# The last stage of a decoder block, turned round: per-layer embedding, its gate and the final norm with tokens on the partitions

## The chip, the core and the metric

The kernel runs on one core of a Trainium2 chip. TensorE multiplies matrices (in the profile PE, and PEld for its weight loads), VectorE (DVE) and ScalarE (ACT) work element by element, GpSimd (POOL) and SyncE (SP) here mostly issue transfers. The metric is the device time of one execution in microseconds (us); the profile gives the span from the first to the last instruction of one profiled execution.

## What is computed

One layer on 512 tokens of width 1024, all in float32. The change touches only the last lines of the reference:

```
    h = h + 0.5 * swiglu(rms_norm(h, g_ffn2), w_ffn2_gate, w_ffn2_up, w_ffn2_down)

    gate = jax.nn.sigmoid(rms_norm(h, g_ple) @ w_ple_gate)     # (512, 1024) @ (1024, 1024)
    h = h + gate * (p @ w_ple_proj)                            # (512, 256) @ (256, 1024)
return rms_norm(h, g_final)
```

## The kernel before

All activations lie with features on the partitions: h is eight tiles (`KD = 8`) of 128 features x 512 tokens in the big tile `gx`. A float32 product is made of three matmuls of the faster type fp32r, because each operand is split into a high part rounded to fp32r and a remainder (names ending in h and l): `mm3` (lines 337 to 339) issues high x high, high x low, low x high. In a matmul row of the profile the first name is the operand that moves and the second the one that is loaded as weights: `pg<-xsh,pgh 128*128 128x256` moves 256 tokens of `xsh` past 128 x 128 of `pgh`.

Weights come in slabs of 128 x 1024 floats (512 KB). `slab_order` writes their order down; `slab(key)` hands one out and on the way issues the loads some seven slabs ahead (`load_one`, from SP's queue, line 190) and the splits two slabs ahead (`split_one`). For the gate matrix, key `("pg", m)`, a split is two halves of 512 columns: ACT writes `pgh` (line 304), DVE subtracts to give the half of `wl` (line 305). Loads wait for a free buffer among 19, which the matmuls of the second feed-forward give back. Every engine takes its instructions in the order in which the program writes them.

The stage around the change runs after the second feed-forward's last down-projection (tiles `pd`). While that ends, `into(V_GP, gs, gnorm, h)` makes `gs` (`xsh`, `xsl`: h times the gain g_ple, split) and sums the squares of h in `gnorm`. Then:

1. The projection `pp` (L337 to L339 with 512 tokens moving): 8 output tiles of 128 features, 6 matmuls each, copied out of PSUM by ACT (L1089). Inside it `gnorm.by_token()` finds 1/rms of each token with small matmuls against `mean` (L450) and a dozen tiny DVE operations (L456 to L462).
2. The gate, in two halves of 256 tokens, 8 output tiles `m` each, 24 matmuls of 256 columns per tile. The 1/rms of a token varies along a row here, so it is spread over all partitions by one matmul (`on_all`, L471 and L477: tile `R`) and multiplied in by DVE (`gate`, L1122) ahead of the Sigmoid (L1123).
3. `add_on`, one tile later: times `pp` (L1129), plus h (L1130), times the gain g_final into `hg` (L1131), squares for the final norm (L428, L436, L1139).
4. `fnorm[half].by_token(...)` for the final norm, `turn_out`: 32 transposes of 128 x 128 of `hg` on PE (L1101) to put tokens on the partitions, and `put_out`: times 1/rms out of PSUM by DVE (L1110) and ACT (L1108), 256 KB a transfer to `out` from SP's queue (L1112). The first half's part lies beside the second half's matmuls; the second half's comes after the last matmul.

The splits of the gate's slabs stand in the same two instruction streams as steps 2 and 3: at tile `m` of the first half the program writes the split of slab `m + 2`, then the work on tile `m`, then `add_on` of tile `m - 1`.

Of the kernel before, what the change touches and what calls it, by code (L numbers as in the profile page):

```python
# [12 lines left out]
I32 = mybir.dt.int32  # L13
# [114 lines left out]
def block_kernel(ctx: ExitStack, tc: tile.TileContext, a, out):  # L128
# [7 lines left out]
    psum = ctx.enter_context(tc.tile_pool(name="psum", bufs=1, space=PSUM))  # L136
    ctx.enter_context(tc.manual_schedule())
# [26 lines left out]
    def source(key):  # L164
# [21 lines left out]
    def fetch(*srcs, first_=False):  # L186

        r, at = W("wh", F32R) if first_ else W("wr"), 0
        for src in srcs:
            (G if first_ else nc.sync).dma_start(r[:, at:at + src.shape[-1]], src)  # L190
            at += src.shape[-1]
        return r[:, :at]
# [226 lines left out]

    class Norm:  # L420
# [18 lines left out]
        def by_token(self, lo=0, hi=NB, more=()):  # L439
            n = hi - lo  # L440
            every = [self.acc] + list(more)
# [3 lines left out]
            ps = [bank("ss") for _ in range(n if more else 1)]  # L445
            pairs = [(i, b) for b in range(n) for i in range(len(every))]
            if more:
                pairs.sort()
            for i, b in pairs:
                PE.matmul(ps[b % len(ps)][:, b:b + 1], every[i][:, b * P:(b + 1) * P], mean[:, 0:1], start=i == 0,  # L450
                          stop=i == len(every) - 1)
            m, y, t = (small.tile([P, NB], F32, name=name(q), tag="nt" + q, bufs=2) for q in "myt")
            m, y, t = m[:, :n], y[:, :n], t[:, :n]
            w = n // len(ps)
            for i, p in enumerate(ps):
                V.tensor_scalar(m[:, i * w:(i + 1) * w], p[:, i * w:(i + 1) * w], EPS, None, op0=OP.add)  # L456
            V.tensor_scalar(t.bitcast(I32), m.bitcast(I32), 1, None, op0=OP.logical_shift_right)
            V.tensor_scalar(y.bitcast(I32), t.bitcast(I32), -1.0, MAGIC, op0=OP.mult, op1=OP.add)
            for _ in range(3):
                V.tensor_mul(t, m, y)  # L460
                V.scalar_tensor_tensor(t, t, -0.5, y, op0=OP.mult, op1=OP.mult)
                V.scalar_tensor_tensor(y, t, 1.5, y, op0=OP.add, op1=OP.mult)  # L462
            if n == NB:
# [611 lines left out]

    pTh, pTl = slab(("pT",))
    pp = []
    for j in range(2):
        wh, wl = slab(("pp", j))
        for i in range(4):  # L1080
            if j and i == 1:
                gnorm.by_token()
            p = bank("pp")
            for kk in range(2):
                c = slice((2 * i + kk) * P, (2 * i + kk + 1) * P)
                z = slice(kk * S, (kk + 1) * S)
                mm3(p, wh[:, c], wl[:, c], pTh[:, z], pTl[:, z], kk == 0, kk == 1)
            t = T("pp")
            A.activation(t, p, AF.Copy)  # L1089
            pp.append(t)  # L1090
    pTh = pTl = wh = wl = None
    H = S // 2
    kept = []
    fin = []

    def turn_out(half, m):

        for b in range(2):
            if m % 4 == 0:
                fin[half][b].append(bank("py"))  # L1100
            PE.transpose(fin[half][b][m // 4][:, (m % 4) * P:(m % 4 + 1) * P], hg[half][m][:, b * P:(b + 1) * P], ident)  # L1101

    def put_out(half, r):
        for b in range(2):
            for c in range(2):
                y = T("y")
                if c:
                    A.activation(y, fin[half][b][c], AF.Copy, scale=r[:, b:b + 1])  # L1108
                else:
# [133 lines left out]
```

## Time and profile before

| | |
|---|---|
| time, median of 3 runs (lowest to highest) | 1329.42 us (1329.3 to 1331.38) |
| the profiled execution: its own time | 1330.73 us |
| the profiled execution: span | 1329.0 us |
| mean granted TensorE clock over the span | 0.996 of 2.4 GHz |
| PE busy, share of the span | 99% |
| DVE, ACT, POOL busy, share of the span | 63%, 52%, 17% |

Times in the profile count from the start of the span. Busy time of a matmul is a model that overlaps its neighbours; how fast matmuls follow one another is read from their start times. The stage of the change covers about the last 75 us: the projection from about 1254, the gate from 1264.86, its last matmul at 1316.41, the end at 1329.0.

### The profile page before, as it was taken

To read this page: it belongs to the slowest core of one execution; us is meant where nothing else is said; L and a number is where in the kernel's file an instruction comes from. 1 tells how busy PE (TensorE), PEld (TensorE's weight loads), DVE (VectorE), ACT (ScalarE), POOL (GpSimd) and SP (SyncE) were. 2 spreads that over 40 slices of the span, in tenths; PEclk is the share of its full clock that TensorE was granted. 3 is DMA by queue.
4 is the path that set the end of the run, shared out by engine and by line. 5 is a ranking of instruction groups with operands and counts; after the bars stand their busy time and mean duration, and the time that the engine had idled before them with its cause. 6 is when DMAs were issued, how large, how long until landed. Compare 5 with 4: busy or idle time off the path is not lost.

```text
span 1329.0 us, 19593 instructions
## 1 busy us (share of the span) xinstructions
PE 1311.4 (99%) x7636; PEld 1168.7 (88%) x7636; DVE 843.8 (63%) x1405; ACT 685.0 (52%) x958; POOL 220.1 (17%) x290
## 2 busy tenths in 40 slices
PE   8999999999999999999999999999999999999997
PEld 6899899898888898989898888888899899898897
DVE  5986467352449877777688956654983366352665
ACT  5567276564522355555464244343676367474553
POOL 3111111112232222222122210001112011111000
PEclk9999999999999999999999999999999999999999
DMA  9678756959888776767577792235479576868601
GB/s 286 140 174 215 198 139 171 244 139 222 199 207 192 166 180 143 157 146 160 133 159 182 169 243 79 95 95 127 115 181 238 164 172 176 225 160 217 178 1 64
DMA packets 78716, 221.05 MB, mean 166 GB/s; under 512 B 8864, under 2 KB 9760, under 8 KB 78624
## 3 DMA queue, kind: packets, MB, share of 16 engines
q0 software_dynamic: 41184, 135.28, 49.3%
q1 hardware_dynamic: 37440, 84.52, 18.6%
q8 instruction: 60, 0.98, 0.3%
q14 instruction: 32, 0.26, 0.1%
HBM read 166.29 MB, written 2.10 MB: 127 GB/s over the span
## 4 chain that ended last, share of the span: by engine, by line
PE 86%; DVE 6%; issue 3%; ACT 2%; DMA 1%; POOL 0%; SPq 0%; DVEq 0%; ACTq 0%; POOLq 0%
PE pd L337 8%; PE pd L339 8%; PE pd L338 8%; PE pa L337 6%; PE pa L339 6%; PE pa L338 6%; PE pg L339 3%; PE pg L338 3%; PE pg L337 3%; PE pq L338 3%; PE pq L337 3%; PE pq L339 3%; PE pv L961 2%; PE pb L337 2%; PE pb L339 2%
## 5 line engine op out<-in xcount | busy, mean ns | idle before, releaser
L264 POOL DMA_DIRECT2D wl<-wr x102 | 89.4, 877 | 508.9 <-ACT wl L261 465.3
L777 DVE SCALAR_TENSOR_TENSOR acc<-glu,taps,acc 128x511 f32<-128x511 f32 (+14 forms) x240 | 165.1, 733 | 0.0
L337 PE MATMUL pd<-hidh,wh 128*128 128x512 f32 x352 | 137.2, 390 | 0.0
L338 PE MATMUL pd<-hidl,wh 128*128 128x512 f32 x352 | 137.2, 390 | 0.0
L339 PE MATMUL pd<-hidh,wl 128*128 128x512 f32 x352 | 137.1, 389 | 0.0
L261 ACT ACTIVATE wl<-wr 128x1024 fp32r<-128x1024 f32 (+1 forms) x102 | 103.9, 1019 | 55.7 <-DMA wr<-in_w_ffn_gate 22.0
L337 PE MATMUL pa<-bh,wh 128*128 128x256 f32 x432 | 122.6, 284 | 1.7 <-ACT p L624 1.7
L339 PE MATMUL pa<-bh,wl 128*128 128x256 f32 x432 | 122.6, 284 | 0.0
L338 PE MATMUL pa<-bl,wh 128*128 128x256 f32 x432 | 122.4, 283 | 0.0
L339 PE MATMUL pg<-xsh,wl 128*128 128x512 f32 (+1 forms) x320 | 111.5, 349 | 0.6 <-DVE wl L305 0.4
L277 ACT ACTIVATE wh<-wr 128x1024 fp32r<-128x1024 f32 (+1 forms) x102 | 103.5, 1014 | 15.4 <-DMA wl<-wr 13.0
L297 DVE TENSOR_TENSOR wl<-s,wh 128x1024 fp32r<-128x1024 f32 x54 | 66.0, 1223 | 68.2 <-ACT wh L296 68.1
L661 DVE SCALAR_TENSOR_TENSOR gx<-pd,gx 128x512 f32<-128x512 f32 x48 | 33.1, 691 | 113.0 <-PE pd L339 112.9
L261 ACT ACTIVATE wl<-wh 128x1024 fp32r<-128x1024 f32 (+1 forms) x84 | 84.3, 1010 | 24.3 <-DMA wh<-in_w_in 15.7
L264 POOL DMA_DIRECT2D wl<-in_w_in x56 | 48.7, 870 | 233.0 <-ACT wl L261 219.5
L337 PEld LDWEIGHTS pa<-bh,wh 128*128 128x128 f32 x432 | 83.0, 192 | 2.1 <-ACT p L624 2.1
L339 PEld LDWEIGHTS pa<-bh,wl 128*128 128x128 f32 x432 | 83.0, 192 | 0.1
L338 PEld LDWEIGHTS pa<-bl,wh 128*128 128x128 f32 x432 | 83.0, 192 | 0.0
L337 PE MATMUL pd<-bh,wh 128*128 128x256 f32 x288 | 82.0, 285 | 0.5 <-ACT p L624 0.4
L338 PE MATMUL pd<-bl,wh 128*128 128x256 f32 x288 | 81.6, 283 | 0.0
L339 PE MATMUL pd<-bh,wl 128*128 128x256 f32 x288 | 81.6, 283 | 0.0
L337 PE MATMUL pg<-xsh,wh 128*128 128x512 f32 x192 | 77.2, 402 | 2.2 <-ACT xsh L357 2.2
(258 smaller groups left out, 3687.0 us busy)
## 6 DMA issues: line engine op xcount, KB each, us to landing
wl<-wr POOLq DMA_DIRECT2D x86, 512.0 KB, 6.7
wh<-in_w_in POOLq DMA_DIRECT2D x56, 512.0 KB, 6.7
wl<-in_w_in POOLq DMA_DIRECT2D x56, 512.0 KB, 5.6
wr<-in_w_ffn_up SPq DMA_DIRECT2D x80, 256.0 KB, 5.0
wr<-in_w_ffn_gate SPq DMA_DIRECT2D x78, 256.0 KB, 5.1
wr<-in_w_ffn_down SPq DMA_DIRECT2D x32, 512.0 KB, 5.7
wr<-in_w_ffn_down SPq DMA_DIRECT2D x16, 384.0 KB, 5.6
wl<-wr POOLq DMA_DIRECT2D x16, 384.0 KB, 6.7
```

The lines of the kernel that those rows point to most:

```text
L261: A.activation(l.bitcast(F32R), h, AF.Copy, scale=-1.0)
L264: G.dma_start(l[:, at:at + src.shape[-1]], src, accum_op=OP.add)
L277: A.activation(h, r, AF.Copy)
L297: V.tensor_sub(l, r, h.bitcast(F32))
L337: PE.matmul(ps, wh, xh, start=start, stop=False, skip_group_check=part)
L338: PE.matmul(ps, wh, xl, start=False, stop=False, skip_group_check=part)
L339: PE.matmul(ps, wl, xh, start=False, stop=stop, skip_group_check=part)
L661: V.scalar_tensor_tensor(resid[m], p, 0.5, resid[m], op0=OP.mult, op1=OP.add)
L777: bg.append(lambda acc=acc, g=g, w=w, s=s: V.scalar_tensor_tensor(acc[:, s:], g[:, :S - s], w, acc[:, s:], op0=OP.mult, op1=OP.add))
L961: PE.matmul(pv[b][:, :384], xh, wh[:, c], start=first_, stop=False)
```

## The change

The same products with the two operands swapped: the activations are loaded as weights (128 tokens at a time) and the weight matrix moves, 512 columns at a time, so the result has tokens on the partitions. There are four blocks `b` of 128 tokens, and for each two column halves `j` of 512 features.

- A slab of the gate matrix is now 128 input features x all 1024 outputs: the same 512 KB, read as 1024 pieces of 512 bytes (eight to a partition) where it was 128 rows of 4 KB.
- Block 0 runs over the slabs as the outer loop, both `j` side by side, six matmuls to a slab; the split parts stay in SBUF for blocks 1 to 3.
- 1/rms is now one number per partition: `by_token(diag=False)` leaves out the `diag` tiles, `on_all` goes, and the Sigmoid reads PSUM and takes 1/rms as its scale. DVE's multiplication by `R` goes.
- h is turned instead of the output: 32 transposes of h on PE (`turned`, L1117), eight ahead of block 0, four in the middle of each later unit; DVE adds them from PSUM.
- `close` does a unit's element-wise work; the squares for the final norm come out of one ACT instruction with a sum along the row (`accum_out`). `root` is the tiny chain of DVE operations, once a block; `put_out` of a block stands behind the next block's first unit. The last unit (block 3, j = 1) is cut into two of 256 columns.
- g_final is needed along a row: 1024 numbers are read from the input `gx`, one four-byte element at a time, into a row in DRAM (`row`), and from there copied to all partitions (two tiles `gf` of 256 KB). These three transfers stand in SP's queue.

```
+        if kind == "pg":
+            return a["w_ple_gate"][:, :, key[1] * P:(key[1] + 1) * P].rearrange("m p i -> p m i")
...
+    row, gf = dram.tile([1, D], F32, name="row"), [T("gf") for _ in range(2)]
+    nc.sync.dma_start(row.rearrange("o (c p e) -> o c p e", c=KD, e=1), bass.AP(
+        tensor=a["gx"].tensor, offset=a["gx"].offset + V_GF, ap=[[0, 1], [1, KD], [V_DW + S, P], [1, 1]]))
+    for c in range(2):
+        nc.sync.dma_start(gf[c], row[0:1, c * S:(c + 1) * S].partition_broadcast(P))
...
-                mm3(p, wh[:, c], wl[:, c], pTh[:, z], pTl[:, z], kk == 0, kk == 1)
+                z = slice(kk * S + b * P, kk * S + (b + 1) * P)
+                PE.matmul(p, pTh[:, z], wh[:, kk], start=kk == 0, stop=False)
+                PE.matmul(p, pTl[:, z], wh[:, kk], start=False, stop=False)
+                PE.matmul(p, pTh[:, z], wl[:, kk], start=False, stop=kk == 1)
...
+    def products(units, ks=range(KD)):
+        for k in ks:
+            for b, j, z, p in units:
+                xh, xl = (t[:, b * P:(b + 1) * P] for t in gs[k])
+                wh, wl = (t[j][:, z] for t in kept[k])
+                p = p[:, :z.stop - z.start]
+                PE.matmul(p, xh, wh, start=k == 0, stop=False)
+                PE.matmul(p, xl, wh, start=False, stop=False)
+                PE.matmul(p, xh, wl, start=False, stop=k == KD - 1)
+
+    def turned(b, j, z):
+        p = bank("hT", "cv")
+        for i in range(z.start // P, z.stop // P):
+            PE.transpose(p[:, i * P - z.start:(i + 1) * P - z.start], h[4 * j + i][:, b * P:(b + 1) * P], ident)
+        return p
+
+    def close(b, j, z, p, hT):
+        w = z.stop - z.start
+        t, u = T("gt")[:, :w], T("hg")[:, :w]
+        A.activation(t, p[:, :w], AF.Sigmoid, scale=r[:, b:b + 1])
+        V.tensor_mul(t, t, pp[b, j][:, z])
+        V.tensor_add(t, t, hT[:, :w])
+        part = tiny("part", 1)
+        A.activation(u, t, AF.Square, scale=D ** -0.5, accum_out=part)
+        V.tensor_mul(t, t, gf[j][:, z])
+        if b in sums:
+            V.tensor_add(part, part, sums[b])
+        else:
+            V.tensor_scalar(part, part, EPS, None, op0=OP.add)
+        sums[b] = part
...
+    def put_out(b):
+        y = sums.pop(b)
+        for i, (t, c, w) in enumerate(done.pop(b)):
+            if i % 2:
+                V.tensor_scalar(t, t, y, None, op0=OP.mult)
+            else:
+                A.activation(t, t, AF.Copy, scale=y)
+            nc.sync.dma_start(out[b * P:(b + 1) * P, c:c + w], t)
+
+    units = [(0, j, whole, bank("pg")) for j in range(2)]
+    hTs = [turned(*u[:3]) for u in units]
+    for k in range(KD):
+        kept.append(slab(("pg", k)))
+        products(units, (k,))
+    for u, t in zip(units, hTs):
+        close(*u, t)
+    root(0)
+    for b in range(1, NB):
+        for j in range(2):
+            for z in (slice(0, 256), slice(256, 512)) if b == NB - 1 and j else (whole,):
+                u = b, j, z, bank("pg")
+                products([u], range(4))
+                hT = turned(*u[:3])
+                products([u], range(4, KD))
+                close(*u, hT)
+                if j == 0:
+                    put_out(b - 1)
+        root(b)
+    put_out(NB - 1)
```

ACT's instructions from the last copies of the projection on, before:

```order
L1089 ACTIVATE pp_11737<-pp_11730 128x512
L304 ACTIVATE pgh_11740<-wr_11589 128x512
L304 ACTIVATE pgh_11743<-wr_11589 128x512
L477 ACTIVATE R_11775<-R_11773 128x512
L1123 ACT_TABLE_LOAD
L1123 ACTIVATE gt_11777<-gt_11777 128x256
L304 ACTIVATE pgh_11781<-wr_11622 128x512
L304 ACTIVATE pgh_11784<-wr_11622 128x512
L1123 ACTIVATE gt_11814<-gt_11814 128x256
L1131 ACTIVATE hg_11817<-gt_11777,gx 128x256
L428 ACTIVATE sq_11821<-gt_11777 128x256
L304 ACTIVATE pgh_11824<-wr_11631 128x512
```

And now, from the same place (six more rows of L310 follow, then the table load):

```order
L1099 ACTIVATE pp_11740<-pp_11733 128x512
L310 ACTIVATE pgh_11755<-wr_11591 128x512
L310 ACTIVATE pgh_11758<-wr_11591 128x512
L310 ACTIVATE pgh_11770<-wr_11630 128x512
L310 ACTIVATE pgh_11773<-wr_11630 128x512
L310 ACTIVATE pgh_11785<-wr_11639 128x512
L310 ACTIVATE pgh_11788<-wr_11639 128x512
```

The splits of slabs 2 to 7 now follow one another, and the gate's own work on ACT (and, in the same way, on DVE) stands behind the last of them.

SP's queue from the projection's second slab on, before:

```order
L190 DMA wr_11494<-in_w_ple_proj 128x1024
L190 DMA wr_11523<-in_w_ple_gate 128x1024
L190 DMA wr_11556<-in_w_ple_gate 128x1024
L190 DMA wr_11589<-in_w_ple_gate 128x1024
L190 DMA wr_11622<-in_w_ple_gate 128x1024
L190 DMA wr_11631<-in_w_ple_gate 128x1024
```

And now:

```order
L196 DMA wr_11496<-in_w_ple_proj 128x1024
L194 DMA wr_11525<-in_w_ple_gate 128x8x128
L194 DMA wr_11558<-in_w_ple_gate 128x8x128
L194 DMA wr_11591<-in_w_ple_gate 128x8x128
L1080 DMA row<-in_gx 1024x1x1
L1083 DMA gf_11621<-row 128x512
L1083 DMA gf_11622<-row 128x512
L194 DMA wr_11630<-in_w_ple_gate 128x8x128
L194 DMA wr_11639<-in_w_ple_gate 128x8x128
```

The three transfers for g_final have come in between the loads of gate slabs 2 and 3; the two `gf` copies read what the `row` copy writes, so SP waits for its landing before it issues them, and the loads of slabs 3 to 7 stand behind.

## Rows read from the trace of the kernel before

**Rows 1.** Busy time of each engine by stretch (us from the start of the span; then the granted clock of TensorE, the mean busy share of the 16 DMA engines, and GB/s).

```profile
1245.00:1264.90 19.90, 19.90 (x93) 16.45 (x93) 15.49 (x33) 12.40 (x20) 0.00 (x0) 1.00 0.32 107
1264.90:1275.00 10.10, 10.10 (x81) 9.62 (x80) 4.11 (x8) 6.27 (x12) 0.00 (x0) 1.00 0.00 1
1275.00:1285.00 10.00, 9.75 (x79) 9.35 (x79) 6.96 (x15) 5.73 (x13) 0.00 (x0) 1.00 0.01 2
1285.00:1296.00 11.00, 10.56 (x86) 10.16 (x86) 8.39 (x22) 6.19 (x15) 0.00 (x0) 1.00 0.01 1
1296.00:1316.50 20.50, 20.50 (x176) 20.50 (x175) 11.73 (x37) 8.55 (x20) 0.00 (x0) 1.00 0.12 46
1316.50:1322.90 6.40, 3.61 (x30) 3.05 (x28) 5.15 (x21) 1.43 (x3) 0.00 (x0) 1.00 0.05 19
```

**Rows 2.** The chain of work that ended last (start, duration, what): the projection's matmuls of 512 columns, the first and the last of 23 that follow one another.

```profile
1254.77 0.23 PE pp L338
...
1259.76 0.23 PE pp L339
```

**Rows 3.** The timeline: the gate's first matmul of 256 columns, then the first and the last of the 48 at its end, and the transposes behind them.

```profile
1264.86 0.28 PE L337 MATMUL pg<-xsh,pgh 128*128 128x256 f32 x1
...
1310.77 0.28 PE L337 MATMUL pg<-xsh,pgh 128*128 128x256 f32 x1
...
1316.41 0.28 PE L339 MATMUL pg<-xsh,wl 128*128 128x256 f32 x1
...
1316.53 1.47 PE L1101 MATMUL py<-ident,hg 128*128 128x128 f32 x12
```

**Rows 4.** The chain again, from the spreading of 1/rms on: how ACT and DVE hand the splits and the gate's work to one another, and the other PE work inside the gate.

```profile
1267.89 0.87 PE R L471 x2
1268.79 0.60 ACT R L477
1269.40 1.28 ACT L1123
1270.70 0.42 ACT gt L1123
1271.12 0.53 ACT pgh L304
1271.67 1.29 DVE wl L305 x2
...
1299.24 1.24 PE ss L450 x12
...
1303.46 0.87 PE py L1101 x8
```

**Rows 5.** Groups of instructions of the last 75 us by line and shape (count | busy us, mean ns of one | idle time before them), and one group of the whole run (L895, the attention's sum along a row).

```profile
L305 DVE TENSOR_TENSOR wl<-wr,pgh 128x512 fp32r<-128x512 f32 x16 | 10.3, 688 | 9.3 <-ACT pgh L304 9.3
L1131 ACT ACTIVATE hg<-gt,gx 128x256 f32<-128x256 f32 x16 | 8.2, 510 | 6.6 <-DVE gt L1130 5.8 <-DVE m L456 0.4 <-PE pg L338 0.4
L428 ACT ACTIVATE sq<-gt 128x256 f32<-128x256 f32 x12 | 4.8, 401 | 0.0
L1108 ACT ACTIVATE y<-py,y 128x512 f32<-128x512 f32 x4 | 2.5, 676 | 3.0 <-DVE y L462 3.0
...
L895 ACT ACTIVATION_READ_ACCUMULATOR sc<-sc,nm 128x1 f32 x20 | 3.7, 186 | 0.0
```

**Rows 6.** The timeline: ACT's last copy of the projection and the split of gate slab 2 behind it (x2, so two halves).

```profile
1265.06 0.60 ACT L1089 ACTIVATE pp<-pp 128x512 f32<-128x512 f32 x1 [0.76 <-PE pp L339]
...
1265.55 1.14 ACT L304 ACTIVATE pgh<-wr 128x512 fp32r<-128x512 f32 x2
...
1266.21 1.29 DVE L305 TENSOR_TENSOR wl<-wr,pgh 128x512 fp32r<-128x512 f32 x2 [1.93 <-ACT pgh L304]
```

**Rows 7.** SP's queue: the issues of gate slabs 2, 3, and 6 and 7 (x2).

```profile
1236.85 0.33 SPq L190 DMA_DIRECT2D wr<-in_w_ple_gate  x1
...
1240.93 0.33 SPq L190 DMA_DIRECT2D wr<-in_w_ple_gate  x1
...
1252.98 0.80 SPq L190 DMA_DIRECT2D wr<-in_w_ple_gate  x2
```

**Rows 8.** Transfers (destination and source, count, KB each, median us from issue to landing): the gate's slabs (rows of 4 KB), the output's, the identity (128 pieces of 512 bytes) and `freq` (128 elements of four bytes); the last two run in the first 30 us, in a stretch where the DMA engines were busy throughout.

```profile
wr<-in_w_ple_gate SPq DMA_DIRECT2D x8, 512.0 KB, 4.1
...
out_y<-y SPq DMA_DIRECT2D x8, 256.0 KB, 2.4
...
ident<-in_eye SPq DMA_DIRECT2D x1, 64.0 KB, 5.5
freq<-in_cst SPq DMA_DIRECT2D x1, 0.5 KB, 4.1
```

**Rows 9.** The timeline of the end: the gate's last element-wise work, the tiny chain of the final norm (its first three and last rows), the last scalings, the last two output transfers.

```profile
1316.73 0.43 DVE L1122 TENSOR_TENSOR gt<-pg,R 128x256 f32<-128x256 f32 x1 [1.32 <-PE pg L339]
1317.07 0.41 DVE L1129 TENSOR_TENSOR gt<-gt,pp 128x256 f32<-128x256 f32 x1
...
1320.76 0.17 DVE L457 TENSOR_SCALAR t<-m 128x2 int32<-128x2 int32 x1
...
1322.74 0.16 DVE L462 SCALAR_TENSOR_TENSOR y<-t,y 128x2 f32<-128x2 f32 x1
1322.94 1.41 DVE L1110 TENSOR_SCALAR y<-py,y 128x512 f32<-128x512 f32 x2
1322.99 1.26 ACT L1108 ACTIVATE y<-py,y 128x512 f32<-128x512 f32 x2 [3.04 <-DVE y L462]
...
1324.61 0.90 SPq L1112 DMA_DIRECT2D out_y<-y  x2
```

More of the change, by code (lines that the diff above doesn't have):

```diff
@@ L437, in flush, with by_token @@
                 self.last = None
-        def by_token(self, lo=0, hi=NB, more=()):
-            n = hi - lo
-            every = [self.acc] + list(more)
+        def by_token(self, diag=True):
+            every = [self.acc]
             if self.last is not None:
@@ L444, in by_token @@
                 self.last = None
[L445 to L451, printed above, removed]
-            m, y, t = (small.tile([P, NB], F32, name=name(q), tag="nt" + q, bufs=2) for q in "myt")
[L453 to L463, printed above, removed]
+            p = bank("ss")
+            for b in range(NB):
+                for i, t in enumerate(every):
+                    PE.matmul(p[:, b:b + 1], t[:, b * P:(b + 1) * P], mean[:, 0:1], start=i == 0,
+                              stop=i == len(every) - 1)
+            m, y, t = (small.tile([P, NB], F32, name=name(q), tag="nt" + q, bufs=2) for q in "myt")
+            V.tensor_scalar(m, p[:, :NB], EPS, None, op0=OP.add)
+            rsqrt(m, y, t)
+            if diag:
                 self.diag = T("diag")
@@ L1078, in block_kernel @@
     for j in range(2):
[L1079 to L1082, printed above, removed]
+        wh, wl = (z.rearrange("p (i k m) -> p k i m", i=4, k=2) for z in slab(("pp", j)))
+        for b in range(NB):
+            if j and b == 1:
+                r = gnorm.by_token(diag=False)
             p = bank("pp")
             for kk in range(2):
[L1085 to L1090 removed]
@@ L1091, in block_kernel @@
-    pTh = pTl = wh = wl = None
-    H = S // 2
-    kept = []
[L1094 to L1109, printed above, removed]
-                    V.tensor_scalar(y, fin[half][b][c], r[:, b:b + 1], None, op0=OP.mult)
-                t0 = (2 * half + b) * P
-                nc.sync.dma_start(out[t0:t0 + P, c * S:(c + 1) * S], y)
@@ L1114, in block_kernel @@
-    hg = [[], []]
-    fnorm = [Norm(), Norm()]
-    steps = {}
-    Rg = None
-    def gate(half, m, p):
-        t = T("gt")[:, :H]
-        V.tensor_mul(t, p[:, :H], Rg[:, half * H:(half + 1) * H])
-        A.activation(t, t, AF.Sigmoid)
-        steps[half, m] = t
-    def add_on(half, m):
-        z = slice(half * H, (half + 1) * H)
-        t, u = steps.pop((half, m)), T("hg")[:, :H]
-        V.tensor_mul(t, t, pp[m][:, z])
-        V.tensor_add(t, t, h[m][:, z])
-        A.activation(u, t, AF.Copy, scale=gain(V_GF, m))
-        hg[half].append(u)
-        if m == KD - 2:
-            fnorm[half].flush()
-        if m < KD - 2:
-            fnorm[half].add(t)
-        else:
-            q = T("sq")[:, :H]
-            V.tensor_mul(q, t, t)
-            rest[half].append(q)
```

59 lines of the change are left out of this document (23 added, 36 removed).

## The prediction

> **What bounds the kernel now.** I read the busy time by stretch first [rows 1]. In the projection PE is busy in every microsecond; in the gate (1264.9 to 1316.5) it is nearly so, with small gaps between 1275 and 1296; from 1316.5 on it is half idle, then idle. So two things are for sale: how many PE slots the gate takes, and how long the chain behind the last matmul is. Transfers are not the limit here: their engines are busy 32% of the projection and almost never in the gate.
>
> Next, how fast matmuls follow one another, by start times. With 512 columns: (1259.76 - 1254.77) / 22 = 0.2268 us [rows 2]. With 256 columns: (1316.41 - 1310.77) / 47 = 0.1200 us [rows 3]. Two of 256 thus cost 0.0132 us more than one of 512. The gate begins at 1264.86, and its last slot ends at 1316.41 + 0.12 = 1316.53, where the transposes start [rows 3]: 51.67 us. Of these 384 matmuls take 46.08, the spreading of 1/rms 0.87, the first half's 12 small matmuls 1.24, and its 16 transposes 16 x 0.109 = 1.74 (eight took 0.87) [rows 4]. By subtraction 1.74 us is left, in which PE waited or was slowed. The chain says for what [rows 4]: from 1268.79 to past 1271.67 it runs on ACT and DVE, where the split of a slab stands in line behind the Sigmoid of an earlier tile, and that one waited for `R` and the table load.
>
> Last the end [rows 9]: from PE's last gate slot (1316.53) to the last of the tiny operations (1322.74 + 0.16 = 1322.90) 6.37 us, and from there to the end of the span 6.10 us.
>
> **The change part by part.** *Projection.* The same 48 matmuls of 512 columns, the same copies, the same place for the sums of squares; `diag` (four DVE operations) goes, from an engine that isn't waited for there. Nothing gained; the gate's part begins at 1264.86 as before.
>
> *PE in the gate.* 336 matmuls of 256 become 168 of 512: 40.32 - 38.10 = 2.22 us less; the last 48 keep 256 columns. The spreading goes (0.87 less). The final norm's small matmuls go (1.24 less here). All 32 transposes now lie ahead of the last matmul, not 16: 1.74 more. The 1.74 us of waits go if the splits keep up, which is the next point. Together 4.33 us less: PE's last gate slot ends at 1312.20 instead of 1316.53.
>
> The Trainium skill (TensorE: Matmul & The Clock Gate, Back-to-back issue gap) puts the spacing at N / 2.4 + 2.5 ns, 109 ns for 256 and 216 ns for 512 columns; by it two small ones cost only 3 ns more than one large, the first term would be 0.4 us instead of 2.2, and the sum below 4.4. The rows are slower at both sizes, and more so at 256, so I go by them.
>
> *Splits against block 0.* Eight transposes first, so slab 0's matmuls start at 1264.86 + 0.87 = 1265.73, and each slab then lasts 6 x 0.2268 = 1.36 us (it was 24 x 0.12 = 2.88). ACT can begin with slab 2 where it does now, at 1265.55 behind the last copy; DVE ends slab 2's second half at 1266.21 + 1.29 = 1267.50 [rows 6], and PE wants it at 1265.73 + 2 x 1.36 = 1268.45: 0.95 us to spare. After that nothing else stands between splits on ACT (1.14 us a slab) or DVE (1.29 us a slab), both faster than PE's 1.36, so the reserve grows. Cost nothing, and the 1.74 us of waits go. The cover is thin: every microsecond that a slab comes late beyond it is one on the path. Block 0 ends at 1265.73 + 48 x 0.2268 = 1276.62.
>
> *Element-wise work.* A unit lasts 24 x 0.2268 + 4 x 0.109 = 5.88 us on PE. DVE spends three operations of 0.69 (priced by L305 [rows 5]) on it, half of a tiny chain (2.2 for the block) and half of a scaling of 0.7: 3.5 us. ACT spends about 2: all of it is hidden. The transposes of a unit need the PSUM bank that DVE read two units before; the closest case is block 1's first unit, which turns at 1276.62 + 2.72 = 1279.34, where the addition of block 0's first unit ends at about 1276.1 + 0.7 + 0.7 + 0.7 = 1278.2. One microsecond to spare. ACT's table load (1.28) falls after the last split, at about 1272.5, hidden.
>
> *The three transfers for g_final and the slabs in small pieces.* `row` is issued behind slab 2, at about 1237.3 [rows 7]. SP then stands until it lands, and the loads of slabs 3 to 7 with it. No row shows 1024 elements of four bytes. Below: not shorter than an output transfer, 2.4 us. Above: eight times `freq` as it stands, 8 x 4.1 = 33 us. I take 2.4 + 8 x (4.1 - 2.4) = 16 us [rows 8], an estimate on the high side since the engines were full then. It would land at 1253.3, slab 3 would be issued 0.9 us later (two issues some 0.45 apart ahead of it, as a pair lasts 0.80 and one 0.33 [rows 7]) at 1254.2 instead of 1240.93, and land 4.1 us later at 1258.3; ACT wants it at 1265.55 + 1.14 = 1266.7. Hidden. A slab of rows of 4 KB takes the transfer engines 0.32 x 19.9 / (107 x 19.9 / 524) = 1.57 us [rows 1]. In pieces of 512 bytes: below 1.57, above eight times what `ident` took beyond 2.4 us, 8 x 3.1 = 25 us, again from a crowded stretch. I take twice the lower end, 3.1 us, near it because 3.1 us for one eighth of the bytes was mostly queueing. Slabs 3 to 7 then need 5 x 3.1 + 2.4 = 18 us, to 1272.1, and the last is wanted at about 1271.3 plus its microsecond of reserve: just hidden. So cost nothing, but with both estimates on the high side there is no room left.
>
> The Trainium skill speaks against these edits (DMA: Bandwidth & Descriptors, Rules for kernel authors: a strided last dimension becomes one descriptor per element; Specifications: below 512 bytes a transfer reads, modifies and writes). That is the mechanism of the second rival below; no run here shows it yet.
>
> *Behind the last matmul.* PE to ACT 0.20 (1316.53 to 1316.73 [rows 9]); Sigmoid of 256 with a scale per partition 0.51 (as L1131); hand-over 0.06, product 0.34 and sum 0.43 on DVE, hand-over 0.06; Square 0.40 and reading its sum 0.19 (L428, L895 [rows 5]); hand-over 0.06, times g_final 0.42, adding the parts 0.20; eleven tiny operations 2.14 (1320.76 to 1322.90). Sum 5.01, 1.36 less than now: there is one piece left to close instead of two, and no small matmuls. y is ready at 1317.21. Then ACT scales 512 columns and 256 (0.68 and 0.51, overlapping as now: 1.14 us), SP issues three transfers 0.45 apart from 1318.0, the last at 1318.9; now the last starts at about 1325.1 (1324.61 + 0.90 for a pair, less 0.4), 3.9 us ahead of the end [rows 9]. So the end is at 1322.8: 5.6 us instead of 6.1, 0.5 less.
>
> **Sum.** 4.33 + 1.36 + 0.5 = 6.2 us: the span goes from 1329.0 to 1322.8, and the profiled execution's own time from 1330.73 to 1324.5. That execution lies 1.3 us above the median of the runs; against the median it is 1329.42 - 6.2 = **1323.2 us** (0.47% less). About 0.2%, 2.7 us, is what a measurement of this kernel can tell from no change.
>
> **The rivals.**
> 1. *Slabs 3 to 7 arrive late and pace block 0.* For it: two unseen prices, and a reserve used up by the high estimates. Against: engines busy 32% in the projection and idle in the gate. With 4 us a slab and 16 us for `row`, slab 7 lands at 1254.2 + 20 + 2.4 = 1276.6, 4.2 us too late: 1327.4. Chance 0.12, half of it within 0.2%.
> 2. *The `row` copy alone holds SP (slower than before).* Hidden while slab 3 lands by 1267.7, so up to 1267.7 - 4.1 - 0.9 - 1237.3 = 25 us. From there each microsecond is one on the path; the gain is gone at 31.6 us, and it is slower beyond 0.2% from 34.3. At 36 us: 1323.2 + 11 = 1334. That is just above the 33 us of the upper end, so it takes elements that cost more here, written to DRAM, than those of `freq`. Chance 0.06.
> 3. *PSUM banks or DVE's backlog hold PE in blocks 1 to 3.* With 0.6 us lost in each of six or seven units: 1327. Against: the reserves above. Chance 0.05.
> 4. *A matmul of 512 columns costs the gate as much as two of 256*, 0.240 us, say because activations as weights load less smoothly: 2.2 us of the sum go, 1325.4. Against: the projection's rows of 512 columns load weights of the same size at 0.2268. Chance 0.03. The skill's spacing above would give 1325.0.
>
> **How the numbers follow.** The forecast holds 0.74; its own range, 1321.3 to 1325, comes from the end (a last piece half as large could land 0.5 sooner, hand-overs add up to some 1 us) and from the waits, which were found by subtraction. The range is stretched upward over the first and third rivals to 1327.6, which leaves out rival 2, the rest of rival 1 and a little below. Faster by over 0.2%: 0.74 + 0.03 + half of the first and third rivals 0.08, less 0.02 for a forecast that is merely too good, 0.83. Slower: 0.07, rival 2 and a little of rival 1. Within 0.2%: 0.10.
>
> **What would show it.** Right: the first matmul of 512 columns in the gate near 1265.7, no idle time on PE ahead of the splits in block 0, the last gate matmul ending near 1312.2, the last tiny operation near 1317.2, eight rows of small matmuls on `ss` in the stage instead of 32 (the trace counts each such float32 matmul twice). Rival 1 or 2: ACT's `pgh` waiting for a transfer of `w_ple_gate`, SP long at L1083. Rival 3: transposes `hT` that wait for DVE. Wrong: a spacing of 512 columns over 0.23 us in the gate, or a gate that starts later than 1264.9 because the small pieces hold up the feed-forward's remainders.

## The result and the profile after

| | before | after |
|---|---|---|
| median of 5 runs each, same chip (lowest to highest) | 1329.3 us (1329.15 to 1331.38) | 1322.62 us (1321.92 to 1323.69) |
| ratio, 95% interval | | 0.9945 [0.9932, 0.9957] |
| span of the profiled execution | 1329.0 us | 1320.9 us |
| mean granted TensorE clock | 0.996 | 0.996 |

The change saves 6.7 us; 6.2 were forecast, and the time lies inside the forecast's own range. The two spans differ by 8.1 us, but part of that is not the change's: in the profile after, the gate's stage begins at 1263.90 instead of 1264.86. The four profiled executions of this study whose code ahead of the gate is the changed kernel's begin the stage at 1263.90, 1265.14, 1265.20 and 1265.49, on both sides of the kernel before. So I compare the stage alone, from its first PE instruction to the end of the span: 64.14 us before, 57.0 after, 7.1 less.

Busy time by stretch of the profile after (columns as in [rows 1]):

```profile
1245.00:1264.90 19.90, 19.90 (x97) 16.59 (x96) 13.92 (x28) 12.98 (x22) 0.00 (x0) 1.00 0.68 157
1264.90:1277.00 12.10, 12.10 (x55) 9.99 (x54) 8.27 (x14) 8.02 (x14) 0.00 (x0) 1.00 0.02 5
1277.00:1288.00 11.00, 11.00 (x53) 9.06 (x53) 7.41 (x23) 4.29 (x10) 0.00 (x0) 1.00 0.03 10
1288.00:1300.00 12.00, 12.00 (x58) 9.90 (x57) 6.42 (x20) 3.52 (x8) 0.00 (x0) 1.00 0.21 80
1300.00:1312.00 12.00, 11.69 (x79) 10.52 (x77) 7.66 (x24) 4.27 (x11) 0.00 (x0) 1.00 0.12 44
```

PE is busy in the whole of the gate (the stretch from 1300 ends with its last matmul); the idle 0.25 and 0.44 us of [rows 1] between 1275 and 1296 are gone. The projection's stretch moves more (DMA share 0.68 instead of 0.32) and is as full for PE as before.

Where the gate begins and ends on PE, then ACT's and DVE's splits (the timeline):

```profile
1263.90 1.03 PE L1117 MATMUL hT<-ident,gx 128*128 128x128 f32 x8
1264.69 0.47 PE L1109 MATMUL pg<-pgh,xsh 128*128 128x512 f32 x1
...
1311.41 0.28 PE L1111 MATMUL pg<-wl,xsh 128*128 128x256 f32 x1
```

```profile
1264.59 6.35 ACT L310 ACTIVATE pgh<-wr 128x512 fp32r<-128x512 f32 x12
...
1265.25 7.32 DVE L311 TENSOR_TENSOR wl<-wr,pgh 128x512 fp32r<-128x512 f32 x12 [2.85 <-ACT pgh L310]
```

The gate lasts from 1263.90 to 1311.41 + 0.12 = 1311.53: 47.63 us where it was 51.67. All twelve remaining splits run without a break on ACT, 0.53 each, and on DVE, 0.61 each. Slab 2's second half is done at 1265.25 + 2 x 0.61 = 1266.47, and PE wants it at 1263.90 + 0.87 + 2 x 1.36 = 1267.49: 1.02 us to spare, where the forecast had 0.95. The table load lies behind them, at 1270.96, and PE does not wait for it.

The tail on ACT and DVE (timeline, of the eleven tiny operations the first and the last) and SP's last issues:

```profile
1311.73 0.47 ACT L1124 ACTIVATE gt<-pg,y 128x256 f32<-128x256 f32 x1 [0.49 <-PE pg L1111]
...
1313.22 0.42 ACT L1128 ACTIVATE hg<-gt 128x256 f32<-128x256 f32 x1 [1.01 <-DVE gt L1126]
...
1313.76 0.42 DVE L1129 TENSOR_TENSOR gt<-gt,gf 128x256 f32<-128x256 f32 x1 [0.58 <-ACT hg L1128]
...
1314.29 0.15 DVE L427 TENSOR_SCALAR t<-part 128x1 int32<-128x1 int32 x1
...
1316.21 0.16 DVE L432 SCALAR_TENSOR_TENSOR y<-t,y 128x1 f32<-128x1 f32 x1
...
1317.16 1.30 SPq L1149 DMA_DIRECT2D out_y<-gt  x3
```

y is ready at 1316.37, 4.84 us after PE's last slot, where [rows 9] gave 6.37. From y to the end it is 4.53 us instead of 6.10. Why this last part shrank by so much is seen in what the transfers move at the end, in stretches of the same columns, first before, then after:

```profile
1324.50:1325.50 1.00, 0.00 (x0) 0.00 (x0) 0.00 (x0) 0.00 (x0) 0.00 (x0) 0.50 0.97 361
...
1326.50:1327.00 0.50, 0.00 (x0) 0.00 (x0) 0.00 (x0) 0.00 (x0) 0.00 (x0) 0.50 1.02 381
1327.00:1327.50 0.50, 0.00 (x0) 0.00 (x0) 0.00 (x0) 0.00 (x0) 0.00 (x0) 0.50 0.63 234
1327.50:1329.00 1.50, 0.00 (x0) 0.00 (x0) 0.00 (x0) 0.00 (x0) 0.00 (x0) 0.50 0.00 0
```

```profile
1317.90:1318.40 0.50, 0.00 (x0) 0.00 (x0) 0.00 (x0) 0.00 (x0) 0.00 (x0) 0.50 0.79 291
1318.40:1318.90 0.50, 0.00 (x0) 0.00 (x0) 0.00 (x0) 0.00 (x0) 0.00 (x0) 0.50 1.02 363
1318.90:1319.40 0.50, 0.00 (x0) 0.00 (x0) 0.00 (x0) 0.00 (x0) 0.00 (x0) 0.50 1.05 348
1319.40:1319.90 0.50, 0.00 (x0) 0.00 (x0) 0.00 (x0) 0.00 (x0) 0.00 (x0) 0.50 0.15 47
1319.90:1320.90 1.00, 0.00 (x0) 0.00 (x0) 0.00 (x0) 0.00 (x0) 0.00 (x0) 0.50 0.00 0
```

Before, four transfers of 256 KB keep the engines full for some 2.8 us; after, 0.5 MB do so for some 1.5 us. Ahead of that lie 1.6 us in both kernels (scaling and the first issue), behind it 1.4 to 1.7 us in which nothing is moved. So of the 1.57 us some 1.3 are transfer time and the rest is that quiet end.

Last, SP's queue behind gate slab 2, and the transfers' share while slabs 3 to 7 come (same columns as above):

```profile
1236.33 1.19 SPq L1080 DMA_DIRECT2D row<-in_gx  x1
1250.69 0.83 SPq L1083 DMA_DIRECT2D gf<-row  x2
1251.62 8.67 SPq L194 DMA_DIRECT2D wr<-in_w_ple_gate  x5
```

```profile
1245.00:1250.00 5.00, 5.00 (x24) 4.14 (x23) 3.55 (x5) 3.11 (x5) 0.00 (x0) 1.00 0.00 0
...
1255.00:1260.00 5.00, 5.00 (x28) 4.27 (x26) 4.25 (x7) 4.77 (x10) 0.00 (x0) 1.00 1.13 305
1260.00:1265.00 5.00, 5.00 (x27) 4.20 (x26) 2.03 (x13) 2.10 (x4) 0.00 (x0) 1.00 1.12 273
1265.00:1270.00 5.00, 5.00 (x23) 4.13 (x22) 4.75 (x8) 5.00 (x11) 0.00 (x0) 1.00 0.03 8
```

From the issue of `row` to that of the first `gf` it is 1250.69 - 1236.33 = 14.4 us, in which SP issues nothing else. The transfer engines are not busy with the copy for all of that time: from 1243.2 to 1250.6 the profile has no packet of any transfer. Slab 3 is issued at 1251.62 instead of 1240.93 [rows 7], and the transfer engines are full from 1255 to 1265, where their share was 0.43 and then 0.01 before. Nothing waits for it: ACT, whose splits run without a break from 1264.59, reaches the last slab at 1264.59 + 10 x 0.53 = 1269.9, and by 1265 nearly everything has landed.

### The profile page after: what moved, and what is told of

The parts are those of the page before. It is cut to its first block, busy times and chain, and to the rows that moved or that the text cites. A ratio compares the mean times of both kernels' runs of the same rounds, so it can differ in the third digit from the quotient of the medians.

```text
span 1320.9 us, 19182 instructions
## 1 busy us (share of the span) xinstructions
PE 1304.3 (99%) x7442; PEld 1156.4 (88%) x7442; DVE 838.5 (63%) x1393; ACT 678.3 (51%) x941; POOL 220.1 (17%) x290
## 4 chain that ended last, share of the span: by engine, by line
PE 88%; DVE 5%; issue 3%; ACT 1%; DMA 1%; POOL 0%; SPq 0%; ACTq 0%; DVEq 0%; POOLq 0%
PE pd L343 9%; PE pd L345 9%; PE pd L344 9%; PE pa L343 6%; PE pa L344 6%; PE pa L345 6%; PE pq L344 3%; PE pq L343 3%; PE pq L345 3%; PE pg L344 3%; PE pg L345 3%; PE pg L343 3%; PE pv L964 2%; PE pv L965 2%; PE pv L966 2%
## 5 line engine op out<-in xcount | busy, mean ns | idle before, releaser
L345 PEld LDWEIGHTS pd<-hidh,wl 128*128 128x128 f32 x352 | 66.1, 188 | 14.2 <-DMA wl<-wr 0.4
```

Source lines behind the costliest of these rows:

```text
L345: PE.matmul(ps, wl, xh, start=False, stop=stop, skip_group_check=part)
```

## The experiments

The theory is the prediction's sum: narrower gaps between matmuls on a full PE, no waits for splits, a shorter tail, and transfers that are hidden. All times of before are those of the same series of runs: 1330.67 us for the first four (21 runs), 1330.15 us for the last three (9 runs). A table by stage stands at the end of the section.

### One matmul of 512 columns against two of 256

The changed kernel, with every matmul of 512 columns in the gate as two of 256 that use the same weights (each loads them again) and write the two halves of the same bank:

```
-                PE.matmul(p, xh, wh, start=k == 0, stop=False)
-                PE.matmul(p, xl, wh, start=False, stop=False)
-                PE.matmul(p, xh, wl, start=False, stop=k == KD - 1)
+                n = (z.stop - z.start) // 256
+                for x_, w_, first_, last_ in ((xh, wh, k == 0, False), ...):
+                    for i in range(n):
+                        c = slice(i * 256, (i + 1) * 256)
+                        PE.matmul(p[:, c], x_, w_[:, c], start=first_ and i == 0, stop=last_, ...)
```

> The changed kernel, but each of the gate's 168 matmuls of 512 columns is made as two of 256 (same products, same order of the rest). My theory: the spacing of matmuls is what the gate pays, 0.2268 us for one of 512 and 2 x 0.120 for two of 256, so PE's part of the gate grows from 47.6 by 168 x 0.0132 = 2.2 us to 49.8, and the time lies 4.5 us under the kernel before instead of 6.7. Rival: the width is worth nothing (the gain came from the waits and the end alone): gate 47.6 and 6.7 us under. Second rival: block 0 was in truth paced by the splits, so that longer slabs there hide something: growth of 1.6 or less.

Measured: 1324.45 us, ratio to before 0.9961 [0.9948, 0.9973]. The timeline, the gate's first transposes and its last matmul:

```profile
1265.20 1.03 PE L1118 MATMUL hT<-ident,gx 128*128 128x128 f32 x8
...
1314.60 0.28 PE L1112 MATMUL pg<-wl,xsh 128*128 128x256 f32 x1
```

The gate lasts 1314.72 - 1265.20 = 49.52 us, 1.89 more than in the changed kernel; the tail and the end are the same to 0.01 us. So the width is worth 1.9 us of the 2.2 forecast: 168 matmuls of 512 columns save 11 ns each. The run has 168 matmuls and 168 weight loads more than the changed kernel (7610 of each instead of 7442), so it does not tell the width from the number of weight loads. The Trainium skill (TensorE: Matmul & The Clock Gate, Back-to-back issue gap) gives N / 2.4 + 2.5 ns for an isolated matmul, and says that in a stream of weight loads and matmuls the spacing is set by both. The formula would make it 168 x 2.5 ns = 0.4 us; this run, a stream of fp32r matmuls with a weight load each, shows 1.89, and the measurement decides.

### The row copy made twice

The copy of 1024 four-byte elements is issued twice, one behind the other; all else is as in the changed kernel.

```
-    nc.sync.dma_start(row.rearrange(...), bass.AP(...))
+    for _ in range(2):
+        nc.sync.dma_start(row.rearrange(...), bass.AP(...))
```

> The changed kernel with the copy of g_final into the DRAM row made twice, the second waiting for the first. In the changed kernel SP waited 13.1 us for that copy behind an issue of 1.2, and no engine waited for a gate slab. My theory: that is hidden only by a reserve. Twice 14.3 us puts the landing at about 1265, slab 3 is issued at about 1266, lands 4 to 6 us later, and slabs 4 to 7 follow 1.8 us apart; ACT then waits for the transfers of w_ple_gate and PE in block 0 for the splits, some 5 us (3 to 8): 1 to 3.5 us under the kernel before. Rival: the transfers have no part in it, as many us as one likes are hidden: 6.7 us under. Rival: nothing of it was hidden, the copy costs its full length: 7 to 8 us over the kernel before.

Measured: 1333.04 us, ratio 1.0017 [1.0008, 1.0026]: slower than before by 2.4 us, and so some 9 us above the changed kernel. SP's queue and ACT's splits (timeline), then what PE and its weight loads do, and the granted clock by stretch:

```profile
1237.47 16.01 SPq L1081 DMA_DIRECT2D row<-in_gx  x2
1267.22 0.83 SPq L1084 DMA_DIRECT2D gf<-row  x2
1268.15 9.52 SPq L194 DMA_DIRECT2D wr<-in_w_ple_gate  x5
```

```profile
1276.03 1.15 ACT L310 ACTIVATE pgh<-wr 128x512 fp32r<-128x512 f32 x2 [9.17 <-DMA wr<-in_w_ple_gate]
...
1283.23 1.15 ACT L310 ACTIVATE pgh<-wr 128x512 fp32r<-128x512 f32 x2 [0.60 <-DMA wr<-in_w_ple_gate]
```

```profile
1276.71 0.80 PE L1110 MATMUL pg<-pgh,xsh 128*128 128x512 f32 x1 [6.53 <-ACT pgh L310]
...
1277.74 0.63 PE L1112 MATMUL pg<-wl,xsh 128*128 128x512 f32 x1
...
1280.72 0.45 PE L1110 MATMUL pg<-pgh,xsh 128*128 128x512 f32 x1
...
1284.64 0.19 PEld L1112 LDWEIGHTS pg<-wl,xsh 128*128 128x128 f32 x1 [0.26 <-DVE wl L311]
```

```profile
1275.00:1280.00 5.00, 3.29 (x8) 2.58 (x9) 2.58 (x4) 2.68 (x5) 0.00 (x0) 0.50 1.20 290
```

This is the second rival's mechanism, brought on by hand: SP held by the copy, slab 3 late, ACT and then PE waiting for it. It also sizes the cover. Slab 3 is issued 16.5 us later than in the changed kernel, and PE stands 6.7 us by its slots (1276.71 less 1270.03, where the last slot ahead of the wait ends; the row's 6.53 counts from the modelled end of that matmul). So some 10 us of the delay were hidden; the stage starts 1.1 us later in this execution, which leaves about 9 us. A single copy of some 23 us would have cost nothing; the forecast put that point at 25.

The price was mis-sized: 3 to 8 us were expected, with a result below the kernel before, and it is 8.86, with a result above. The gate takes 56.49 us (from 1265.03 to 1321.52), 8.86 more than in the changed kernel: 6.7 in which PE stands, and some 2.2 in the rest of block 0. For the latter the rows show two causes that lie over one another. The slabs come (1283.23 - 1276.03) / 4 = 1.80 us apart where PE takes one in 1.36, which alone would cost 4 x 0.44 = 1.8. And behind the 6.5 us without matmuls the granted clock is 0.50, the 1.2 GHz level: matmuls of 512 columns follow one another in (1280.72 - 1277.74) / 7 = 0.426 us until 1280.72, eight or nine of them at 0.20 too much, 1.7 us. Either would nearly fill the 2.2. They do not add up, and by the last slab the slabs hold PE again: its weight load at 1284.64 waits for the split of slab 7. At the full clock PE would have waited there for the same split, so in this run the lower clock cost next to nothing beyond what the slabs cost anyway. The expectation had counted neither.

The second copy also shows how little of a copy's time its packets take. It runs while the transfer engines have nothing else to do: its 1032 packets of under 512 bytes all lie between 1252.8 and 1256.6, and SP goes on only at 1267.22. What the remaining 10.6 us are spent on does not show in the profile.

### Transfers without small pieces

The changed kernel, with the gate's slabs laid out by the host as rows of 4 KB and g_final as a contiguous input row; `row` and its copy go.

```
-            return a["w_ple_gate"][:, :, key[1] * P:(key[1] + 1) * P].rearrange("m p i -> p m i")
+            return a["w_ple_gate"][key[1]]
...
-    nc.sync.dma_start(row.rearrange(...), bass.AP(...))
...
-        nc.sync.dma_start(gf[c], row[0:1, c * S:(c + 1) * S].partition_broadcast(P))
+        nc.sync.dma_start(gf[c], a["gf"][0:1, c * S:(c + 1) * S].partition_broadcast(P))
```

> The changed kernel without the awkward transfers: the gate matrix laid out by the host so that a slab is 128 rows of 4 KB, and g_final given as a contiguous row and copied to all partitions straight from the input, so SP waits for no landing. My theory: both were hidden, so the time is that of the changed kernel, 6.7 us under the kernel before (within 0.7), while the busy share of the transfer engines between 1255 and 1265 falls from over 1 to under 0.5. Rival: the small pieces or SP's wait cost something beside the gate (the feed-forward's remainders share the transfer engines): 1 us or more faster than the changed kernel.

Measured: 1323.44 us, ratio 0.9947 [0.9934, 0.9961], the same as the changed kernel's. The transfers in the two stretches in which they were full:

```profile
1255.00:1260.00 5.00, 5.00 (x24) 4.14 (x23) 4.38 (x6) 4.96 (x10) 0.00 (x0) 1.00 0.52 193
1260.00:1265.00 5.00, 5.00 (x28) 4.24 (x27) 3.17 (x14) 2.52 (x5) 0.00 (x0) 1.00 0.01 3
```

The DMA share falls from 1.13 and 1.12 to 0.52 and 0.01 (under 0.5 was expected), and the stage takes 57.0 us as in the changed kernel. The small pieces cost transfer time, but none of it is on the path: "cost nothing" holds.

### The kernel before, with the splits ahead

The kernel before, with all eight gate slabs taken, and so split, before the gate's first tile:

```
+    kept.extend(slab(("pg", m)) for m in range(KD))
     for half in range(2):
...
-            if half == 0:
-                kept.append(slab(("pg", m)))
```

> The kernel before with one thing moved: all eight slabs of the gate are taken and split ahead of the gate's first half, so that the splits no longer stand between the gate's other work on ACT and DVE; orientation, widths, spreading and the end are as before. My theory: the 1.74 us that PE loses in the first half of the gate (by subtraction) come from that mixing, so the gate shrinks from 51.7 to about 50.0 us and the time lies 1.7 us under the kernel before. Rival: the loss is something else (the slots themselves are longer in places): within 0.5 us of the kernel before. Rival: the first tile's Sigmoid now comes 6 us later and PE runs out of PSUM banks: slower.

Measured: 1329.04 us, ratio 0.999 [0.9981, 0.9998], which is 0.3 to 2.5 us less; 1.7 were expected. By stretch, the transposes behind the gate's last matmul, and what the weight loads of the gate waited for in the kernel before (us in total, times, longest):

```profile
1275.00:1285.00 10.00, 10.00 (x86) 10.00 (x85) 5.90 (x16) 5.29 (x14) 0.00 (x0) 1.00 0.01 2
1285.00:1296.00 11.00, 11.00 (x94) 11.00 (x94) 6.16 (x16) 3.86 (x10) 0.00 (x0) 1.00 0.01 1
```

```profile
1314.87 1.36 PE L1101 MATMUL py<-ident,hg 128*128 128x128 f32 x11
```

```profile
PEld pg L339 <- DVE wl L305: 0.9, 2, 0.4
PEld pg L337 <- ACT pgh L304: 0.6, 2, 0.4
```

PE is full where [rows 1] had 9.75 of 10 and 10.56 of 11 us, and the gate lasts from 1264.90 to 1314.87, 49.97 us: 1.70 less than before. The 1.74 us that the prediction found only by subtraction are there, and it is the order of splits and Sigmoid that makes them. [rows 1] show only 0.69 us of them as idle time; a matmul of 256 columns is given 0.28 us of busy time at a spacing of 0.12, so a wait of up to 0.16 us leaves no gap there. The weight loads show 1.5 us of waits for splits, and none of them is left with the splits ahead.

### The last unit uncut

The changed kernel with block 3's second half as one unit of 512 columns:

```
-            for z in (slice(0, 256), slice(256, 512)) if b == NB - 1 and j else (whole,):
+            for z in (whole,):
```

> The changed kernel, with its last half of the last block as one unit of 512 columns instead of two of 256: 8 matmuls of 256 columns more become 4-column-pairs fewer, that is 24 matmuls of 512 in place of 48 of 256, and the output of the last block leaves in two transfers instead of three. Theory (the cut pays by a shorter chain behind the last matmul): the gate's matmuls end about 0.3 us earlier (24 x (2 x 0.1200 - 0.2268) = 0.32), but Sigmoid, product, residual, square and the product with g_final behind the last matmul each stand over 512 columns instead of 256, some 0.2 to 0.27 us more each, so the row that gives y comes 1.0 to 1.3 us later after the last matmul. In sum 0.7 to 1.0 us later than the changed kernel, about -5.8 us against the kernel before. Rival (the transfers behind y, not the chain, set the end, and two transfers end sooner than three): the same as the changed kernel, -6.7.

Measured: 1325.29 us, ratio 0.996 [0.9948, 0.9973]. The timeline from the last matmul to y:

```profile
1312.66 0.39 PE L1111 MATMUL pg<-wl,xsh 128*128 128x512 f32 x1
...
1318.92 0.16 DVE L432 SCALAR_TENSOR_TENSOR y<-t,y 128x1 f32<-128x1 f32 x1
```

The gate (from 1265.49 to 1312.66 + 0.23 = 1312.89) is 0.23 us shorter, the way to y is 6.19 us, 1.35 longer, and y to the end 0.11 shorter: the stage is 1.0 us longer. The theory holds, at the upper end of its numbers and for y just above them (1.0 to 1.3 were expected). The medians cannot tell this kernel from the changed one (the interval is 3.6 to 6.9 us under the kernel before). Of the 1.36 us that the prediction gives the tail, about as much hangs on this cut; with 512 columns the tail would have stood at 6.19, hardly below the 6.37 of before.

### Half of the last block's output

The changed kernel, whose three last transfers write only half of their columns; the other halves of the last block's output are left out:

```
-            nc.sync.dma_start(out[b * P:(b + 1) * P, c:c + w], t)
+            n = w // 2 if b == NB - 1 else w
+            nc.sync.dma_start(out[b * P:(b + 1) * P, c:c + n], t[:, :n])
```

> The changed kernel, but the three output transfers of the last block write only the left half of their columns; the right halves of the last 128 tokens' output are left out. The number of transfers and all arithmetic are as in the changed kernel. Theory (the stretch from the last transfer's issue to the end follows the bytes behind y): 0.25 MB less at some 400 GB/s, so about 0.6 us less from y to the end than the changed kernel's 4.53 us. Rival (that stretch is a fixed latency of one transfer and of the program's end): 4.5 us as before, within 0.2.

Measured: 1323.03 us, ratio 0.9946 [0.9931, 0.9961]. What the transfers move at the end:

```profile
1318.90:1319.40 0.50, 0.00 (x0) 0.00 (x0) 0.00 (x0) 0.00 (x0) 0.00 (x0) 0.50 0.29 100
1319.40:1319.90 0.50, 0.00 (x0) 0.00 (x0) 0.00 (x0) 0.00 (x0) 0.00 (x0) 0.50 0.81 253
1319.90:1320.40 0.50, 0.00 (x0) 0.00 (x0) 0.00 (x0) 0.00 (x0) 0.00 (x0) 0.50 0.48 139
```

From y (1317.61) to the end it is 4.29 us, 0.24 less than after, not the 0.6 expected, and within what this part varies by between executions of the same last steps (4.53, 4.53, 4.54, and 4.94 in the kernel with the copy made twice). The expectation missed. The rows show that 0.25 MB now take about as long as 0.5 MB, at 253 GB/s or less and with the engines at most 0.81 busy, so it is no longer bytes that set this stretch. Three issues 0.44 us apart (0.88 for two) would explain it; so would pieces of 1 KB and 512 bytes where they were 2 KB and 1 KB. This run does not tell the two apart. In the kernel before, the engines are full at 361 to 381 GB/s for most of the stretch. That bytes made the step from before to after thus rests on the rows of transfers of these two kernels; this experiment did not confirm it.

### A shorter tail

The kernel without small pieces, with the last piece's product with g_final out of the chain ahead of y: it is done together with the scaling, and the three last scalings are shared out anew.

```
-        V.tensor_mul(t, t, gf[j][:, z])
+        last_ = b == NB - 1 and z.stop == S and j
+        if not last_:
+            V.tensor_mul(t, t, gf[j][:, z])
...
-            if i % 2:
+            if i == 2:
+                V.scalar_tensor_tensor(t, t, y, gf[1][:, c - S:c - S + w], op0=OP.mult, op1=OP.mult)
+            elif i % 2 == (b < NB - 1):
                 V.tensor_scalar(t, t, y, None, op0=OP.mult)
```

> The changed kernel with the gate's slabs laid by the host as rows of 4 KB and g_final as a row of its own (as in e3_clean), and with the last piece's product with g_final taken out of the chain in front of y: it is done with the scaling by y in one instruction behind it; of the last block's three scalings the 512 columns go to VectorE, and one piece of 256 each to ScalarE and VectorE. Theory (the tail is a chain of small instructions, and taking one out shortens it by what that one takes): y comes 0.3 us earlier after the last matmul; the scalings end about 0.3 us earlier, since ScalarE has one piece instead of two (0.56 each); the whole is 0.3 to 0.6 us less than the changed kernel, -7.0 to -7.3 us against the kernel before. Rival (the product with g_final lies beside the wait for ScalarE's accumulator, and the end is set by the transfers): no difference that can be told from e3_clean, -7.0.

Measured: 1321.8 us, ratio 0.9941 [0.9928, 0.9953], the lowest median here. The timeline of its end:

```profile
1311.07 0.28 PE L1108 MATMUL pg<-wl,xsh 128*128 128x256 f32 x1
...
1313.42 0.16 DVE L1130 TENSOR_TENSOR part<-part,part 128x1 f32<-128x1 f32 x1 [0.57 <-ACT hg L1125]
...
1315.54 0.16 DVE L432 SCALAR_TENSOR_TENSOR y<-t,y 128x1 f32<-128x1 f32 x1
...
1316.25 1.31 SPq L1150 DMA_DIRECT2D out_y<-gt  x3
```

The addition of the parts now follows ScalarE directly, and y comes 4.51 us after the last slot instead of 4.84: 0.33, as expected. The rest of the end takes 4.30 us, 0.23 less, which is within what that part varies by. In the stage that is 56.4 us against 57.0. The medians' intervals overlap those of the changed kernel, so the times can't tell the two; the profile shows the 0.33, and whether the 0.23 is the edit's stays open.

### All of them by stage

Us; the first column from the start of the span, the others lengths. For the two kernels in the order of before the gate begins with its first matmul, for the others with the transposes.

| | gate begins | gate on PE | last slot to y | y to the end | stage |
|---|---|---|---|---|---|
| before | 1264.86 | 51.67 | 6.37 | 6.10 | 64.1 |
| before, splits ahead | 1264.90 | 49.97 | 6.36 | 6.07 | 62.4 |
| after | 1263.90 | 47.63 | 4.84 | 4.53 | 57.0 |
| 512 as two of 256 | 1265.20 | 49.52 | 4.84 | 4.54 | 58.9 |
| row copy twice | 1265.03 | 56.49 | 4.84 | 4.94 | 66.3 |
| no small pieces | 1265.39 | 47.63 | 4.85 | 4.53 | 57.0 |
| last unit uncut | 1265.49 | 47.40 | 6.19 | 4.42 | 58.0 |
| half of the last output | 1265.14 | 47.63 | 4.84 | 4.29 | 56.8 |
| shorter tail | 1263.56 | 47.63 | 4.51 | 4.30 | 56.4 |

Read down a column: the gate on PE and the way to y come out equal to 0.01 us wherever their code is equal, so a single profile tells tenths of a microsecond there, where the medians can't tell two. From y to the end it does not: equal code gives 4.53 to 4.94.

## Why the prediction was right, point by point

- **PE in the gate**: 47.34 forecast, 47.63 measured. The unit with its 24 matmuls and four transposes takes 5.93 us, not 5.88 (0.229 us a matmul, still under the 0.23 that the prediction named as a sign of being wrong): the rate taken from the projection was a little too good for the gate, and the width is worth 1.9 us instead of 2.2. The waits (1.74) were real, as the splits put ahead show with 1.70. The 1/rms spread, the small matmuls and the transposes were not tested one by one; the sum leaves 4.04 - 1.89 - 1.70 = 0.45 us for the three together, where 0.87 + 1.24 - 1.74 = 0.37 were forecast. The fourth rival (no gain from the width) is answered by the run with two of 256. The formula that the prediction quotes from the Trainium skill (TensorE: Matmul & The Clock Gate, Back-to-back issue gap) is given there for an isolated matmul, which the prediction does not say.
- **Splits against block 0**: as put; a reserve of 1.02 us against 0.95, no wait.
- **Element-wise work and banks**: the transposes of block 1's first unit begin at 1278.42, and DVE's addition that frees their bank ends at 1276.74 + 0.69 = 1277.43, 0.99 us ahead, where one microsecond was forecast. PE waited for no bank, so the third rival did not come.
- **The transfers**: hidden, as put, but their prices were estimates of uneven quality. The row copy took 14.4 us where 16 were taken, inside bounds of 2.4 and 33. That the number came so close is luck: the estimate scaled `freq`'s time by its elements and called it high because the engines had been full, but the copy takes as long on idle engines (waits of 13.9 and 13.7 us in the kernel with two), and for more than half of that time they have nothing to move. A slab in pieces of 512 bytes takes 1.8 us (by the landings in the kernel with the copy made twice), not 3.1: the value taken was too high, and the fear that no room was left was not borne out. From its issue to its landing a slab takes 7.8 us in the median, not the 4.1 carried over from rows of 4 KB, which the cover took in. The first rival would have needed 4 us a slab; slabs paced block 0 only once they were issued 16 us late. The second rival's mechanism exists and its place was right, with the point from which it decides at some 23 us instead of 25; it needed a copy 9 us longer than the one that was there. On the strided copy, the Trainium skill (DMA: Bandwidth & Descriptors, Rules for kernel authors) speaks of one descriptor per element, and the trace agrees: 1032 packets of under 512 bytes for the 1024 elements. These packets are not what took the 14.4 us, though. What decided here is that only loads with 9 us of cover stood behind it.
- **Behind the last matmul**: 5.01 forecast, 4.84 measured. Square with the reading of its sum takes 1313.76 - 1313.22 = 0.54 (0.65 counted), product with g_final and the addition of the parts 1314.29 - 1313.76 = 0.53 (0.62 counted): the ends overlap a little (the reading of the sum starts at 1313.54, ahead of Square's end at 1313.64).
- **From y to the end**: the term that was mis-sized. 5.6 us forecast (0.5 less than before), 4.53 measured (1.57 less). The step that failed is "now the last starts at about 1325.1 ..., 3.9 us ahead of the end": these 3.9 us were carried over as if fixed, but before they hold the rest of 1 MB that leaves at 381 GB/s until about 1327.3, and after there are only 0.5 MB. After the change the last issue starts at about 1318.0, 2.9 us ahead of the end. The forecast's own range named this ("a last piece half as large could land 0.5 sooner"); it was twice that, since the whole last block is half as large, not its last piece alone.

The stage's terms then add up to 4.04 + 1.53 + 1.57 = 7.1 us against 6.2, and the median's 6.7 lies between; its interval, 5.7 to 9.0 us, holds both. The two errors, the width too dear by 0.3 and the end too cheap by 1.1, go in opposite directions, so the forecast of the sum is a little better than its terms. What is left between 7.1 and 6.7 is less than the starts of the stage vary (1.6 us), and that the measured 6.7 lies as near to 6.2 as it does is in part luck.

## What to carry to other kernels

Where one engine is full in a stage, count its slots and get the spacing of each width from start times in the trace; and look for other engines' work that stands in line ahead of the operands it waits for, since that costs slots even where little idle time shows. An ugly transfer is priced by what stands behind it in its queue and by the moment at which that is wanted, and doubling it in an experiment measures the cover. The time from the last result to the end is not a constant: part of it is the bytes that are still to go, so it shrinks when the last step is cut finer, until something other than bytes sets it.

## What the runs showed of the hardware that I had not expected

- A transfer of 1024 elements of four bytes takes 14 us (14.4 in the changed kernel from issue to the next issue; waits of 13.9 and 13.7 for the two copies that followed one another), 3.5 times what the 128 elements of `freq` took in [rows 8], not eight times. Most of it is not traffic: of the second copy, on idle engines, every packet lies in the first 3.8 us.
- After PE had stood 6.53 us the granted clock was 0.50 (1.2 GHz), and matmuls of 512 columns went from 0.227 to 0.426 us apart until 1280.72, after which they were back at 0.227. These slower matmuls sum to 1.7 us; here they cost next to nothing, since the splits would have held PE to the same end at the full clock. In the kernel before, where PE never stood for long in the gate, the granted clock stays 1.00 throughout [rows 1].
- Short waits for an operand are mostly hidden in the busy time: 0.69 us idle in [rows 1] for the 1.70 us that the earlier splits gave back. The waits of the weight loads show more of them, 1.5 us.
- Halving the bytes of the last three transfers from 0.5 to 0.25 MB saved 0.24 us at most: they moved at 253 GB/s or less, with the engines at most 0.81 busy. Whether the issues, 0.44 us apart, or the smaller pieces set that is not shown.
